# Raw weights and meta products of the first gate pair moved behind its pre-split loads; residual and result stores issued from ScalarE's queue

## The chip, the cores and the metric

The kernel runs on one core of one Trainium2 chip. The metric is the device time of one execution in microseconds: before the change 2130.71 us, the median of three runs (2130.59 to 2131.08). The five engines of the core each take their instructions in a fixed order: TensorE (PE) multiplies matrices, VectorE (DVE), ScalarE (ACT) and GpSimd (POOL) work element by element, SyncE (SP) issues DMA transfers. Any of SP, ACT and POOL can issue a DMA; the issuing instruction stands in that engine's order like any other, and what is behind it waits for it.

## The reference

One layer of a bidirectional encoder is applied to two requests with the same weights, a long one of 1024 tokens and a short one of 512; 16 learned meta tokens stand ahead of each. Cut to what matters here:

```python
D_MODEL = 1024; SEQ = 1024; DEC_SEQ = 512; N_META = 16; D_FF = 2816

def mixer_sublayer(x, ...):                 # two attention groups A and B
    ...
    return x + concat([oa, ob]) @ w_out     # output projection and residual

def conv_glu_sublayer(x, g_ffn, w_ff_gate, w_ff_up, conv_w, conv_b, w_ff_down):
    n = rms_norm(x, g_ffn)
    gate = n @ w_ff_gate
    pad = jnp.pad(gate, ((0, 0), (1, 1), (0, 0)))
    gate = pad[:, :-2] * conv_w[0] + pad[:, 1:-1] * conv_w[1] + pad[:, 2:] * conv_w[2] + conv_b
    return x + (jax.nn.gelu(gate, approximate=False) * (n @ w_ff_up)) @ w_ff_down

def trunk(x, ...):
    h = jnp.concatenate([meta, x], axis=1)
    h = mixer_sublayer(h, ...)
    h = conv_glu_sublayer(h, ...)
    return rms_norm(h, g_final)[:, N_META:]
```

All of it is in float32. The convolution runs over the tokens, so the first real token needs the gate value of the last meta token too.

## The kernel before

**Products.** Activations lie with the 1024 features (or 2816 inner features, 22 column tiles of 128) on the partitions and the tokens along the free axis. A float32 product is made of three faster ones: each operand is split into a rounded part `hi` (a cast on ACT, L114) and the rest `lo` (a subtraction on DVE or POOL, L115), and `mm3` multiplies hi by hi, lo by hi and hi by lo (L121 to L123). So a weight that comes raw from memory costs ACT and DVE a split before PE can use it; some weights are written to memory in split form earlier, while PE is busy with attention, and are then loaded in two parts, `w_hi` and `w_lo`: six of the eight column tiles of w_out (`wo`) and the first pair of column tiles of the gate weight (`wg`).

**Order.** The program is written as Python generators for the two requests, interleaved by hand; a scheduler of the framework, which simulates the engines, then fixes the order in which each engine takes its instructions, from the dependences and from the order of the program. DMA transfers signal their end over one of eight semaphores, taken in turn: a DMA waits until the one before it on its semaphore has landed.

**The stretch that the change touches** has three parts.

1. `mixer_out_long` is the output projection of the long request, in three parts of 340 to 344 tokens (`PARTS`, one piece of each half of the request). For each part it loads the attention output `m` and splits it into `xhi` and `xlo`; then for each of the eight column tiles `j` it loads the weight (`wo` in four blocks at L167, or raw w_out at L150, which is cast on ACT), loads the residual `res` (L712), multiplies (24 matmuls), adds the residual on DVE (L728), **stores the new residual `h`** (L729, read again much later), and adds up squares for the norm (L583; the last two as `sq_p` at L734). The norm itself and the operands that the next stage needs (`combine`: L657, L103 to L107, then casts `x_hi`, `t_hi` and subtractions) are delayed and run inside the next part; those of the third part run inside the gate stage.
2. Beside it the short request ends: `finish` in `conv_glu` scales the result and **stores it as `yT`** (L845), 16 stores of 128 KB in two groups of eight.
3. `conv_glu_long` makes gate and up of the long request, two column tiles (a pair) at a time. Each pair's gate is a Winograd-like scheme of seven products instead of eight (`winograd`), each of 12 matmuls; the first pair takes its operands pre-split from `wg` (L920, five pairs of buffers) and is made in two chunks of tokens, 342 and then 170 in each half, so that the first chunk can start before the third part of the projection is normalised. So the first pair has fourteen products and fourteen loads of two blocks.

**The meta products.** The gate value of the last meta token is made apart, from the *raw* gate weights: for each of the two column tiles ACT multiplies the eight blocks of the weight by the token's normalised values `x0` (`prod`, L970, eight instructions), DVE adds them up (`acc`, L972), and a matmul with two columns sums over the partitions (L989); its result goes into column 0 of `gate` (L990). The convolution starts on ACT (L996, without column 0), two DVE steps add the neighbours (the first one reads column 0), and the GELU follows (L1001). Then come the up products, from raw w_up weights that are split on chip. The raw gate weights have two buffers (`w_f`), shared with the raw w_out tiles of the projection; w_up has two of its own.

In the code before, the raw gate weights of every pair are loaded and the meta products made ahead of that pair's products:

```python
raw = [load_whole(wp, g, g.w_gate[f0 + i]) for i in range(2)]
first_sums = []
for i in range(2):
    ...
for c0, cw in ((0, first), (first, H - first)) if f0 == 0 else ((0, H),):
    for i, half, ps, rest in winograd(g, wp, up, x, raw, c0, cw, g.wg if f0 == 0 else None):
        ...
```

## Time and profile before

| | |
|---|---|
| median of three runs | 2130.71 us |
| the profiled execution | 2127.9 us |
| its span in the profile | 2126.1 us |
| mean granted clock of PE | 0.989 |
| PE busy | 2040.4 us, 96% of the span |
| DVE busy | 1725.0 us, 81% |
| ACT busy | 1156.0 us, 54% |
| POOL busy | 560.8 us, 26% |
| DMA | 296.31 MB, mean 139 GB/s |

The profile is of one execution, and its times are microseconds from the start of its span. In the rows that follow, `PE ps_mm L121 <- DMA w_hi<-wg` is a wait: the PE instruction of line 121 that writes `ps_mm` waited for the DMA that brings `w_hi` from `wg`. A row with a time first is an instruction (or a run of like ones, `x8`): its start, how long it took, engine and line, its output and input, and in brackets how long its engine had been idle before it, and what ended that. `SPq` is SP's queue, where a row is a DMA being issued, not the transfer. A row `1350.00:1375.00` is a stretch of the span: its length, the busy time of each engine with its count of instructions, the clock granted to PE (1.00 is full speed), and the share and rate of the DMA engines.

### The profile page before, as it was taken

Reading aid. Unit: us, or ns where it says so; the run is one execution under the profiler, and the core shown is the slowest. Engines: PE = TensorE matmul, PEld = TensorE weight load, DVE = VectorE, ACT = ScalarE, POOL = GpSimd, SP = SyncE. Lnnn points to the kernel's source line nnn. Section 1 sums busy time; section 2 is a strip of 40 time slices with the busy share of each in tenths; the row PEclk is TensorE's granted clock in tenths of the full one; section 3 lists DMA queues with packets and bytes.
Section 4 is the critical chain, followed back from the end, with each engine's and each line's share of the span. In section 5 each row is a group of like instructions: output and inputs, shape, how many; then the busy total and the mean of one; then the engine's idle time right before and its main releaser. Section 6 shows DMA issues by size and latency. Waiting matters only on the chain.

```text
span 2126.1 us, 35236 instructions
## 1 busy us (share of the span) xinstructions
PE 2040.4 (96%) x12302; PEld 1822.3 (86%) x12302; DVE 1725.0 (81%) x3786; ACT 1156.0 (54%) x2253; POOL 560.8 (26%) x494
## 2 busy tenths in 40 slices
PE   6999999998999999999999999988999999999998
PEld 6988888997887989999989999987887777778877
DVE  6878889767879788888998885578778878879886
ACT  6635566544567556666666765345444444435454
POOL 4653233453112000000000000421544444330112
PEclk9999999999999999999999999999999999999999
DMA  7563435457621322223352225996322232247443
GB/s 255 176 203 130 119 111 171 153 178 236 209 79 56 105 75 67 74 82 118 104 187 88 86 97 147 276 290 217 107 100 90 101 113 84 94 167 260 119 126 127
DMA packets 171426, 296.31 MB, mean 139 GB/s; under 512 B 21456, under 2 KB 90608, under 8 KB 170736
## 3 DMA queue, kind: packets, MB, share of 16 engines
q1 hardware_dynamic: 171248, 294.05, 42.5%
q8 instruction: 97, 1.59, 0.3%
q14 instruction: 81, 0.66, 0.1%
HBM read 211.13 MB, written 82.85 MB: 138 GB/s over the span
## 4 chain that ended last, share of the span: by engine, by line
PE 76%; DVE 12%; DMA 4%; issue 3%; ACT 2%; POOL 1%; SPq 0%; DVEq 0%; ACTq 0%; POOLq 0%
PE ps_mm L121 17%; PE ps_mm L123 17%; PE ps_mm L122 17%; PE ps_t L456 5%; PE ps_s L431 3%; PE ps_s L432 3%; PE ps_s L122 2%; PE ps_s L123 2%; PE ps_s L121 2%; DVE p L433 2%; PE ps_o L471 2%; DVE w_lo L115 1%; PE ps_o L470 1%; DVE acc L972 1%; DMA m<-oT 1%
## 5 line engine op out<-in xcount | busy, mean ns | idle before, releaser
L121 PE MATMUL ps_mm<-xhi,w_hi 128*128 128x258 f32 (+3 forms) x1264 | 383.1, 303 | 12.3 <-ACT xhi L114 5.6
L122 PE MATMUL ps_mm<-xlo,w_hi 128*128 128x258 f32 (+3 forms) x1264 | 378.4, 300 | 0.3 <-POOL xlo L115 0.3
L123 PE MATMUL ps_mm<-xhi,w_lo 128*128 128x258 f32 (+3 forms) x1264 | 377.1, 299 | 0.3 <-DVE w_lo L115 0.3
L433 DVE TENSOR_SCALAR_CACHE_REDUCE p<-ps_s 114x344 f32<-114x344 f32 (+4 forms) x562 | 257.8, 489 | 28.1 <-PE ps_s L432 16.8
L114 ACT CAST pt_hi<-ps_t 128x512 fp32r<-128x512 f32 (+6 forms) x360 | 169.6, 484 | 180.8 <-PE ps_t L456 153.3
L121 PEld LDWEIGHTS ps_mm<-xhi,w_hi 128*128 128x128 f32 x1264 | 239.6, 190 | 18.3 <-ACT xhi L114 7.8
L438 ACT ACTIVATE p<-p,nm 114x1040 f32<-114x1040 f32 (+5 forms) x212 | 214.8, 1013 | 70.5 <-DVE nm L436 69.3
L115 DVE TENSOR_TENSOR w_lo<-w_f,w_hi 128x1024 fp32r<-128x1024 f32 (+1 forms) x182 | 195.2, 1080 | 67.3 <-ACT w_hi L114 66.8
L122 PEld LDWEIGHTS ps_mm<-xlo,w_hi 128*128 128x128 f32 x1264 | 240.0, 190 | 1.9 <-POOL xlo L115 0.8
L123 PEld LDWEIGHTS ps_mm<-xhi,w_lo 128*128 128x128 f32 x1264 | 239.4, 190 | 1.2 <-DVE w_lo L115 0.5
L114 ACT CAST w_hi<-w_f 128x1024 fp32r<-128x1024 f32 (+1 forms) x199 | 167.4, 856 | 79.3 <-PE ps_mm L122 52.2
L115 DVE TENSOR_TENSOR pt_lo<-ps_t,pt_hi 128x512 fp32r<-128x512 f32 (+4 forms) x312 | 172.0, 562 | 42.5 <-ACT pt_hi L114 40.9
L115 POOL TENSOR_TENSOR a_lo<-gate,a_hi 128x256 fp32r<-128x256 f32 x44 | 43.1, 981 | 540.9 <-ACT a_hi L114 521.0
L431 PE MATMUL ps_s<-k,q 128*114 128x348 f32 (+4 forms) x552 | 182.7, 336 | 3.2 <-DVE p L433 3.0
L456 PE MATMUL ps_t<-ident,p 128*128 128x128 f32 (+7 forms) x1188 | 182.4, 269 | 0.9 <-DVE nm L436 0.5
L121 PE MATMUL ps_s<-xhi,w_hi 128*128 128x256 f32 (+4 forms) x480 | 148.2, 311 | 23.2 <-DVE t L333 7.7
L432 PE MATMUL ps_s<-k,q 128*114 128x348 f32 (+4 forms) x552 | 170.3, 313 | 0.0
L456 PEld LDWEIGHTS ps_t<-ident,p 128*128 128x128 f32 (+7 forms) x1188 | 139.9, 135 | 29.1 <-issue 6.8
L123 PE MATMUL ps_s<-xhi,w_lo 128*128 128x256 f32 (+4 forms) x480 | 147.0, 307 | 3.2 <-DMA w_lo<-wo 3.0
L122 PE MATMUL ps_s<-xlo,w_hi 128*128 128x256 f32 (+4 forms) x480 | 148.7, 311 | 1.2 <-DVE xlo L115 0.5
L122 PE MATMUL ps_mm<-t_lo,w_hi 128*128 128x512 f32 (+2 forms) x368 | 142.8, 388 | 1.4 <-DVE t_lo L115 1.4
L121 PE MATMUL ps_mm<-t_hi,w_hi 128*128 128x512 f32 (+2 forms) x368 | 142.8, 388 | 0.0
(273 smaller groups left out, 5269.7 us busy)
## 6 DMA issues: line engine op xcount, KB each, us to landing
w_f<-w_gate SPq DMA_DIRECT2D x46, 512.0 KB, 3.4
w_f<-w_up SPq DMA_DIRECT2D x44, 512.0 KB, 3.3
w_f<-w_in SPq DMA_DIRECT2D x36, 512.0 KB, 4.0
a_f<-act SPq DMA_DIRECT2D x62, 256.0 KB, 2.7
w_f<-w_down SPq DMA_DIRECT2D x22, 512.0 KB, 3.4
act<-a_t SPq DMA_DIRECT2D x44, 256.0 KB, 2.1
a<-w_down SPq DMA_DIRECT2D x40, 256.0 KB, 5.4
w_hi<-wo SPq DMA_DIRECT2D x36, 256.0 KB, 5.2
```

Of the source, the lines that this page charges most:

```text
L114: return (nc.scalar.copy(hi, src).ins, (lo_engine or nc.vector).tensor_tensor(out=lo, in0=src, in1=hi.bitcast(F32), op=ALU.subtract).ins)
L115: (lo_engine or nc.vector).tensor_tensor(out=lo, in0=src, in1=hi.bitcast(F32), op=ALU.subtract).ins)
L121: nc.tensor.matmul(ps, lhsT=whi, rhs=xhi, start=start, stop=False)
L122: nc.tensor.matmul(ps, lhsT=whi, rhs=xlo, start=False, stop=False)
L123: return nc.tensor.matmul(ps, lhsT=wlo, rhs=xhi, start=False, stop=stop).ins
L431: nc.tensor.matmul(ps, lhsT=q[0], rhs=k[:, c0:c0 + cw], start=True, stop=False)
L432: nc.tensor.matmul(ps, lhsT=q[1], rhs=k[:, c0:c0 + cw], start=False, stop=True)
L433: nc.vector.tensor_scalar(out=p[:, c0:c0 + cw], in0=ps, scalar1=HD ** -0.5, scalar2=-3.0e38, op0=ALU.mult, op1=ALU.max, accum_out=mx[:, i: ...
L438: g.last_exp = nc.scalar.activation(p, p, AF.Exp, bias=nm, accum_out=l).ins
L456: nc.tensor.transpose(tps[:, c:c + M], p[:, k0:k0 + kw], g.ident[:M, :M])
L470: nc.tensor.matmul(o, lhsT=v[:, i, :], rhs=hi, start=i == 0, stop=False)
L471: nc.tensor.matmul(o, lhsT=v[:, i, :], rhs=lo, start=False, stop=False)
```

## The change

Three things are edited.

1. The stores of `h` (L729, 24 of them, or eight for each part) and of `yT` (L845, 16) are issued from ACT instead of SP.
2. The raw loads and the meta products become a function, `load_gate`. For every pair but the first it is called where the code stood before. For the first pair it is called after the fourteen products, and what it issues is held, by `behind`, until the last `wg` load has been issued (`g.last_load`). `winograd` no longer gets the raw weights there, which it never used.
3. The raw w_up weights of the first pair are loaded in the same place, behind `wg`, instead of after the GELU in the program's order.

```diff
@@ mixer_out_long @@
-                nc.sync.dma_start(out=halves(g.h[j], o, w),
-                                  in_=h[:, j, :2 * w].rearrange("p (x t) -> p x t", x=2))
+                nc.scalar.dma_start(out=halves(g.h[j], o, w),
+                                    in_=h[:, j, :2 * w].rearrange("p (x t) -> p x t", x=2))
@@ conv_glu, finish @@
-                    nc.sync.dma_start(out=yv[:, k + 1 - ob:k + 1, c0:c0 + cw], in_=y)
+                    nc.scalar.dma_start(out=yv[:, k + 1 - ob:k + 1, c0:c0 + cw], in_=y)
@@ winograd @@
-    a11, a12, a21, a22 = (w[:, i * H:(i + 1) * H] for w in raw for i in range(2))
+    if pre is None:
+        a11, a12, a21, a22 = (w[:, i * H:(i + 1) * H] for w in raw for i in range(2))
+    else:
+        a11 = a12 = a21 = a22 = s2 = None
...
-                nc.sync.dma_start(out=tl.bitcast(F32), in_=pre[i, part, :, half * H:(half + 1) * H])
+                g.last_load = nc.sync.dma_start(out=tl.bitcast(F32), in_=pre[i, part, :, half * H:(half + 1) * H]).ins
@@ conv_glu_long @@
+    def load_gate(f0):
         raw = [load_whole(wp, g, g.w_gate[f0 + i]) for i in range(2)]
-        first_sums = []
+        sums = []
         for i in range(2):
             prod = up.tile([P, KT, P], F32, name="prod", tag="prod", bufs=1)
             for k in range(KT):
                 nc.scalar.activation(prod[:, k], raw[i][:, k * P:(k + 1) * P], AF.Copy, scale=g.x0[:, k:k + 1])
             acc = up.tile([P, P], F32, name="acc", tag="acc")
             nc.vector.tensor_reduce(out=acc, in_=prod.rearrange("p k c -> p c k"), axis=AX.X, op=ALU.add)
-            first_sums.append(acc)
+            sums.append(acc)
+        return raw, sums
+
+    for f0 in range(0, NFF, 2):
+        gate = up.tile([P, 2, N + 1], F32, name="gate", tag="gate", bufs=1)
+        if f0:
+            raw, first_sums = load_gate(f0)
...
+        if f0 == 0:
+            with behind(g, g.last_load):
+                raw, first_sums = load_gate(f0)
+                raw_up = [load_whole(up, g, g.w_up[f0 + i], "w_f2") for i in range(2)]
...
-        raw = [load_whole(up, g, g.w_up[f0 + i], "w_f2") for i in range(2)]
+        raw = raw_up if f0 == 0 else [load_whole(up, g, g.w_up[f0 + i], "w_f2") for i in range(2)]
```

How the engines' orders change is shown at three places. Lines behind the change have 13 more than before (L989 becomes L1002, L996 becomes L1009), L970 becomes L972 and L935 becomes L938. First ACT, from the norm of the projection's third part (L103) to the first casts of the up weights (`w_hi<-w_f_19441`), before:

```order
L103 ACTIVATE rs_y<-ps_s,eps 128x340
L970 ACTIVATE prod<-w_f,x_18439 128x128 x8
L104 ACTIVATE rs_y<-rs_y 128x340
L105 ACTIVATE rstd<-rs_y 128x340
L970 ACTIVATE prod<-w_f,x_18439 128x128 x8
L114 CAST x_hi<-h 128x4x170
L935 COPY u<-ps_mm 128x342
L114 CAST x_hi<-h 128x4x170 x2
L970 ACTIVATE prod<-w_f,x_18439 128x128 x8
L114 CAST t_hi<-h 128x4x170 x4
L935 COPY u<-ps_mm 128x170
L114 CAST w_hi<-w_f_19441 128x512 x2
```

The same engine and place after the change, from the casts of the third part's operands on, with the two conv starts (L1009) and the first casts of the up weights (`w_f_19423`):

```order
L114 CAST t_hi<-h 128x4x170 x4
L938 COPY u<-ps_mm 128x170
L972 ACTIVATE prod<-w_f,x_18439 128x128 x8
L1009 ACTIVATE act<-gate,vec 128x1024 x2
L114 CAST w_hi<-w_f_19423 128x512 x2
L972 ACTIVATE prod<-w_f,x_18439 128x128 x8
L1003 ACTIVATE gate<-ps_mm 128x1
L114 CAST w_hi<-w_s 128x512 x2
```

The two groups of eight meta products stood ahead of and behind the norm; they now stand after it, after the copy from the second chunk's first product, and the second group behind both conv starts and the first two casts of the up weights. (The third group in the rows of before belongs to the second pair.)

Second PE, where the last gate product (`t_hi`, 170 tokens) is followed by the first up product (`x_hi`, 512 tokens), before:

```order
L122 MATMUL ps_mm<-t_lo,w_hi 128x170
L989 MATMUL ps_mm<-ones_d,acc 128x2 x2
L123 MATMUL ps_mm<-t_hi,w_lo 128x170
L121 MATMUL ps_mm<-t_hi,w_hi 128x170
```

And after:

```order
L121 MATMUL ps_mm<-t_hi,w_hi 128x170
L122 MATMUL ps_mm<-t_lo,w_hi 128x170
L123 MATMUL ps_mm<-t_hi,w_lo 128x170
L1002 MATMUL ps_mm<-ones_d,acc 128x2 x2
L121 MATMUL ps_mm<-x_hi,w_hi 128x512
L122 MATMUL ps_mm<-x_lo,w_hi 128x512
```

The two sums over the partitions stood inside the last gate product, ten matmuls before its end; now they stand between that product and the first up product, so that nothing of up can start on PE before both `acc` are made.

Third ACT at the second group of eight result stores, in the projection's third part, before:

```order
L839 ACTIVATE y<-h,gain 128x256 x2
L583 ACTIVATE sq<-h 128x344
L114 CAST xhi<-m 128x340
L114 CAST x_hi<-h 128x4x170 x3
L114 CAST xhi<-m 128x340
L583 ACTIVATE sq<-h 128x344
```

And after:

```order
L114 CAST xhi<-m 128x340
L839 ACTIVATE y<-h,gain 128x256 x2
L845 DMA yT<-y 128x256 x8
L729 DMA h_100<-h 256x1x172
L583 ACTIVATE sq<-h 128x344
L729 DMA h_100<-h 256x1x172
L114 CAST xhi<-m 128x340 x3
L114 CAST w_hi<-w_f 128x512
```

Eight stores of `y` and two of `h` now stand in ACT's order between the scaling of the short request's result (L839) and the casts of the third part's activations (`xhi`).

More of the change, by code (lines that the diff above doesn't have):

```diff
@@ L961, in conv_glu_long @@
     first = PARTS[-1][0]
-    for f0 in range(0, NFF, 2):
-        gate = up.tile([P, 2, N + 1], F32, name="gate", tag="gate", bufs=1)
+    def load_gate(f0):
         raw = [load_whole(wp, g, g.w_gate[f0 + i]) for i in range(2)]
-        first_sums = []
+        sums = []
         for i in range(2):
@@ L972, in conv_glu_long @@
             nc.vector.tensor_reduce(out=acc, in_=prod.rearrange("p k c -> p c k"), axis=AX.X, op=ALU.add)
-            first_sums.append(acc)
+            sums.append(acc)
[4 more added lines that the diff above has]
+            raw, first_sums = load_gate(f0)
         for c0, cw in ((0, first), (first, H - first)) if f0 == 0 else ((0, H),):
-            for i, half, ps, rest in winograd(g, wp, up, x, raw, c0, cw, g.wg if f0 == 0 else None):
+            for i, half, ps, rest in winograd(g, wp, up, x, raw if f0 else None, c0, cw, None if f0 else g.wg):
                 t0 = 1 + half * H + c0
```

## The prediction

> **What bounds the kernel now.** I read the 25 us windows around the changed code first, then the waits of TensorE (PE) there, the chain, and the queue of SyncE (SP).
>
> ```profile
> span 2126.1 us, 35236 instructions
> ...
> core 0: us, PE busy (x) PEld busy (x) DVE busy (x) ACT busy (x) POOL busy (x), PEclk, DMA share, GB/s
> 1350.00:1375.00 25.00, 24.24 (x162) 23.18 (x161) 16.67 (x32) 11.34 (x27) 9.16 (x11) 1.00 0.92 283
> 1375.00:1400.00 25.00, 21.38 (x122) 20.52 (x122) 19.15 (x33) 10.83 (x24) 8.27 (x9) 0.93 0.93 290
> 1400.00:1425.00 25.00, 20.37 (x108) 18.05 (x107) 15.51 (x25) 8.79 (x18) 3.71 (x4) 0.93 0.85 266
> 1425.00:1450.00 25.00, 22.79 (x130) 21.24 (x129) 19.44 (x25) 14.15 (x32) 6.84 (x5) 0.93 0.95 314
> 1450.00:1475.00 25.00, 20.95 (x148) 19.55 (x148) 24.97 (x40) 14.28 (x32) 2.73 (x2) 1.00 0.65 232
> 1475.00:1500.00 25.00, 25.00 (x108) 20.10 (x107) 20.47 (x25) 11.44 (x17) 13.14 (x10) 1.00 0.32 110
> ```
>
> PE is the bound: full from 1475 on. What can be won or lost lies in the four windows from 1375 to 1475, where PE is idle for 3.6 + 4.6 + 2.2 + 4.1 = 14.5 us and its granted clock falls to 0.93. These are the end of the output projection of the long request and the first gate pair. What PE waits for there, from 1320 to 1480:
>
> ```profile
> engine line waited for: us in total, times, longest us
> PE ps_s L121 <- DMA w_hi<-wo: 4.1, 3, 2.5
> PE ps_s L123 <- DMA w_lo<-wo: 3.0, 3, 1.7
> PE ps_s L657 <- ACT sq_p L734: 2.2, 2, 1.3
> PE ps_mm L121 <- DMA w_hi<-wg: 1.9, 1, 1.9
> ...
> PE ps_mm L123 <- DMA w_lo<-wg: 0.7, 1, 0.7
> ```
>
> Mostly weights that come late: `wo` (pre-split w_out) and `wg` (pre-split first gate pair). The queue says why, in SP's rows and one of PE:
>
> ```profile
> 1370.55 5.78 SPq L845 DMA_DIRECT2D yT<-y  x8
> 1376.42 0.52 SPq L729 DMA_DIRECT2D h<-h  x1
> 1377.03 0.56 SPq L167 DMA_DIRECT2D w_hi<-wo  x1
> 1381.91 0.43 PE L121 MATMUL ps_s<-xhi,w_hi 128*128 128x344 f32 x1 [2.53 <-DMA w_hi<-wo]
> ...
> 1406.07 0.33 SPq L150 DMA_DIRECT2D w_f<-w_out  x1
> 1413.30 0.33 SPq L150 DMA_DIRECT2D w_f<-w_gate  x1
> ...
> 1445.70 4.86 SPq L150 DMA_DIRECT2D w_f<-w_gate  x2
> ```
>
> SP issues in order. Eight result stores hold it from 1370.55 to 1376.33, the next weight block goes out at 1377.03, and PE stands 2.53 us for it. From 1406.4 to 1413.3 SP issues nothing: the raw gate weight waits for a free buffer. From 1445.70 it is held 4.86 us by the raw weights of the second gate pair, which wait until the meta products have read the first pair; the `wg` loads behind them are those that PE then misses.
>
> **What the change removes.** All 40 stores leave SP, and the four raw loads of the first pair (w_gate, w_up) go behind the last `wg` load. Two terms.
>
> *Term 1, the output projection.* Its stretch as a whole, and two short windows after idle gaps:
>
> ```profile
> 1362.00:1438.00 76.00, 67.21 (x390) 63.35 (x389) 59.04 (x94) 33.13 (x67) 24.17 (x24) 0.96 0.90 278
> 1382.00:1387.00 5.00, 5.00 (x22) 4.95 (x23) 2.94 (x5) 2.42 (x5) 0.91 (x2) 0.66 1.02 375
> 1410.00:1414.00 4.00, 4.00 (x18) 4.00 (x17) 0.69 (x1) 0.62 (x1) 0.00 (x0) 0.57 0.18 70
> ```
>
> Bound by PE: 76 − 67.2 = 8.8 us idle, and twice 0.34 × 5 = 0.43 × 4 = 1.7 us of slow clock, together 12.2 us. Bound by the transfers: 278 GB/s for 76 us are 21.1 MB; the two raw gate loads (1.05 MB) go, leaving 20.1 MB. At the unchanged share of 0.90 that takes 72.2 us, 3.8 less; at a share of 1.0 (309 GB/s) 65 us, 11 less. Whether freeing SP fills the share is not shown before, so the gain lies between 3.8 and 11; I take the middle, 7.4, as only some of the idle transfer time stands at the two places where SP was held.
>
> *The Trainium skill against this.* The skill's page DMA: Bandwidth & Descriptors (Issuing engines are not separate DMA queues) says that DMAs issued from several engines run on the same 16 DMA engines and that spreading them saves only issue time. By that rule the share stays 0.90 and term 1 is 3.8 us, not 7.4. The trace agrees only in part: the share is already 0.85 to 0.95, but what SP loses here is waiting in order (6.9 us before 1413.3), which is more than issue time.
>
> *Term 2, inside the gate pair.* PE's two waits for `wg`, 1.9 + 0.7 = 2.6 us, go: with no raw load ahead of them, each `wg` load is issued when its buffer comes free, and five pairs of buffers cover the landing. The chain before also shows the meta products between the norm and its use:
>
> ```profile
> 1443.34 2.34 ACT prod L970 x8
> 1445.71 2.01 DVE acc L972
> ...
> 1454.68 1.85 DVE acc L972
> ```
>
> These 6.2 us leave DVE's path to the second chunk's operands. They are worth nothing beyond the 2.6 us in the term: what follows them is term 4, which starts from PE's ninth product, and PE's own pace is late next (seven products of 12 matmuls on the first chunk).
>
> **What the change adds.** *Term 3, ACT.* There is no DMA issue on ACT's queue before. The nearest rows are SP's, 0.52 us for an h store; the eight later y stores cost 3.96/8 = 0.50:
>
> ```profile
> 1388.74 3.96 SPq L845 DMA_DIRECT2D yT<-y  x8
> ...
> yT<-y SPq DMA_DIRECT2D x16, 128.0 KB, 3.3
> ```
>
> 40 × 0.5 = 20 us on ACT, which is busy 33.1 of 76 us: as load this is covered. As order it is not. In the changed program the second eight y stores stand ahead of the casts of the last activations (`xhi`) of the projection's third part. A store waits for its y, and for the completion semaphore that it shares with an earlier transfer: stores five to eight share theirs with the first four, and the two h stores behind with later ones. So ACT can stand for two landings, 2 × 3.3 = 6.6 us. PE's cover is the 24 matmuls of that part which need no late cast: 67.21/390 = 0.17 us each, 4.1 us. The price is between 0 and 6.6 us (cover gone); I take 1.4, near the uncovered rest of 2.5 us but below it, since the first eight stores come where nothing urgent is behind.
>
> *Term 4, the handover from gate to up.* Here a wait is added that the trace of before does not have. Its parts, from rows of before:
>
> ```profile
> 1462.60 0.27 PE L121 MATMUL ps_mm<-t_hi,w_hi 128*128 128x170 f32 x1
> 1463.68 0.38 SPq L920 DMA_DIRECT2D w_hi<-wg  x1
> 1464.16 0.39 SPq L920 DMA_DIRECT2D w_lo<-wg  x1
> 1469.83 0.53 PE L989 MATMUL ps_mm<-ones_d,acc 128*128 128x2 f32 x4
> 1471.39 0.43 PE L121 MATMUL ps_mm<-x_hi,w_hi 128*128 128x512 f32 x1
> ...
> w_f<-w_gate SPq DMA_DIRECT2D x4, 512.0 KB, 3.6
> ...
> 1447.76 2.45 ACT L970 ACTIVATE prod<-w_f,x 128x128 f32<-128x128 f32 x8 [1.18 <-DVE acc L972]
> 1471.50 1.25 ACT L996 ACTIVATE act<-gate,vec 128x1024 f32<-128x1024 f32 x1 [1.08 <-issue]
> 1465.68 0.62 ACT L114 CAST w_hi<-w_f 128x512 fp32r<-128x512 f32 x1
> ```
>
> The last `wg` pair needs the buffer of the ninth of fourteen products, done at 1462.60; its second load is out at 1464.55. Before, PE's first up matmul follows at 1471.39, 8.8 us after the ninth product. In the changed program PE has both meta sums (L989) directly ahead of that matmul, and ACT has the first products, two conv starts (L996), two casts, and only then the second products. Counted from the ninth product: last `wg` load issued at 1.95; raw gate weight landed 3.6 later, 5.55; eight products 2.45, 8.0; two conv starts 2 × 1.25, 10.5; two casts 1.24, 11.7; eight products 2.45, 14.2; the sum on DVE 2.01, 16.2; the meta matmuls 0.53, 16.7. So up starts 16.7 − 8.8 = 7.9 us later against its ninth product, and everything behind it with it, for PE is full from there to the end. PE then stands some ten us, which costs at least one slow-clock stretch more, 1.7 us as in the two windows above: 9.6 us.
>
> On that 1.7 the skill's TensorE: Matmul & The Clock Gate (What's actually happening) says that the clock halves after an idle window of about 3.4 us and returns after a busy one. The trace agrees with its size and not with its threshold: 1.7 us were lost after a gap of 2.53 us. By the page's windows 1.7 to 3.4 us would be an estimate for this gap.
>
> **Sum.** −7.4 − 2.6 + 1.4 + 9.6 = +1.0 us. On the profiled execution of 2127.9 us (span 2126.1 and 1.8 around it) that is 2128.9; the median of the runs, 2130.7, lies 2.8 higher, so 2131.7 there, and I say 2132. A measurement of this kernel can tell about 0.2%, 4.3 us, from no change.
>
> **The rivals.**
> - *ACT's queue becomes the new wait: slower.* Third part of the projection, at the second eight y stores. Price 6.6 instead of 1.4: +6.2, 2136.9. It decides when the casts behind the stores end more than 4.1 us after PE has finished the second part. For it: the stores share semaphores with loads of a stretch in which a landing takes 3 to 5 us, and DVE's work on the first part hangs on casts behind them. Against: ACT is idle more than half of the stretch. Chance 0.18.
> - *The transfers bound the projection, whoever issues them: slower.* Term 1 is 3.8: +4.6, 2135.3. For it: the share of 0.90 with 375 GB/s at the best. Against: the share of 0.18 at 1410, which was SP's doing alone. This is the outcome by the skill's rule on issuing engines. Chance 0.14.
> - *SP freed refills everything: faster.* Term 1 is 11 and term 3 nothing: −4.0, 2126.7; at PE's bound of 12.2, −5.2, 2125.5. For it: two long holds of SP each end in a PE wait. Against: it needs a full share for 65 us. Chance 0.18, counting that the raw gate weight may land earlier than I take.
> - *The change does not reach the waits:* the terms 1 and 2 stay near nothing because loads wait for buffers anyway, while term 4 is paid: +9.6 and up, 2140. Against: the 2.53 us wait began while SP stood at the stores. Chance within the slower ones, 0.05 at most.
>
> **How the numbers follow.** My forecast, the two sides cancelling, has 0.50 and is the "same" case. Slower, the first two rivals, 0.32 with the last in it; faster 0.18. Range: down to 2124 (PE's bound of 2125.5, and the slow-clock stretch of 1.7 at the handover not lost), up to 2140 (the last rival), leaving out about 2 in 10.
>
> **What would show each step.** Term 1: no PE wait of 2.53 us for `w_hi<-wo`, no slow clock there, and the end of the projection some 6 us earlier. Term 2: no wait for `wg`. Term 3: ACT idle at L845 rows and PE waiting for `xhi`. Term 4: PE idle for about ten us ahead of L989, released by DVE's `acc`; if that gap is under 4 us, the forecast is wrong on the fast side. If PE is full at the handover or the stretch from 1362 on gets longer, the argument has failed.

## The result and the profile after

The changed kernel took 2143.74 us (median of six runs, 2142.27 to 2146.63) against 2130.89 of the kernel before in runs beside it: a ratio of 1.0059, with a 95% interval of 1.0042 to 1.0075, or 9 to 16 us more. The forecast was 2132 and its range ended at 2140. Executions of one kernel spread widely here (the one before from 2124.6 to 2139.5 in one set of 35), so below a time counts as a ratio with its interval, and a profile is read by stretches and not by its span. The profiled execution of the changed kernel took 2146.12 us, above its median; its span is 2144.3 us.

The 25 us windows of the changed kernel, with the columns of the prediction's first fence:

```profile
1375.00:1400.00 25.00, 19.14 (x115) 17.79 (x114) 15.60 (x30) 8.09 (x19) 7.84 (x10) 1.00 0.92 291
1400.00:1425.00 25.00, 17.49 (x76) 15.78 (x76) 14.22 (x22) 9.96 (x18) 3.22 (x3) 0.80 0.75 243
1425.00:1450.00 25.00, 20.96 (x117) 18.66 (x116) 18.59 (x29) 9.47 (x17) 8.15 (x4) 0.91 0.78 240
1450.00:1475.00 25.00, 24.09 (x167) 23.64 (x166) 18.46 (x34) 7.31 (x12) 0.00 (x0) 0.95 0.75 239
1475.00:1500.00 25.00, 15.62 (x62) 12.54 (x61) 20.46 (x19) 20.32 (x48) 8.67 (x6) 0.73 0.34 124
```

From 1375 to 1425 PE is busy 36.6 us, where it was busy 41.8 before, and from 1475 to 1500 only 15.6 in place of 25. The transfers were to run fuller; their share falls to 0.75. PE's waits in the changed kernel from 1340 to 1490:

```profile
PE ps_mm L1002 <- DVE acc L974: 9.4, 2, 5.0
PE ps_s L657 <- DVE h L728: 4.0, 1, 4.0
PE ps_s L657 <- ACT sq_p L734: 3.0, 2, 1.6
PE ps_s L121 <- DMA w_hi<-wo: 2.7, 2, 2.1
PE ps_s L121 <- ACT xhi L114: 2.7, 1, 2.7
PE ps_s L122 <- DVE xlo L115: 2.6, 2, 2.4
```

Waits for `wo` and `wg` were at the top before; now it is what ACT and DVE make: `acc`, the residual sum `h`, `xhi`, `xlo`.

To compare kernels whose spans have slipped against each other, I cut at two places that all of them have: **the projection stretch** runs from the first norm's sum (L657, 342 columns) to the last sum of the third norm (L657, `sq_p`), and **the gate stretch** from there to the first up matmul of 512 columns. The windows of these two stretches, before:

```profile
1372.97:1441.26 68.29, 57.83 (x325) 53.36 (x323) 51.91 (x81) 28.64 (x54) 18.62 (x17) 0.95 0.92 291
1441.26:1471.39 30.13, 26.08 (x175) 24.92 (x175) 25.58 (x40) 16.88 (x41) 2.94 (x3) 0.95 0.78 278
```

And after:

```profile
1371.32:1448.52 77.20, 59.79 (x324) 54.70 (x322) 52.08 (x84) 28.45 (x57) 22.89 (x21) 0.91 0.83 264
1448.52:1485.88 37.36, 27.06 (x175) 25.90 (x175) 25.48 (x40) 16.94 (x37) 3.03 (x2) 0.82 0.69 228
```

The projection is 8.9 us longer, the gate stretch 7.2. PE does the same work in both (325 and 324 matmuls in the projection). From the start of up to the end there are 3.7 us more (658.4 against 654.7); two of them are slow clock behind the handover, as shown below. The rest, and 1.7 us less ahead of the first cut, came and went from one profile to the next.

**What happens in the projection.** ACT's rows in the changed kernel, around the two groups of `yT` stores (`ACTq` is ACT's queue, as SPq was SP's):

```profile
1373.25 4.85 ACTq L845 DMA_DIRECT2D yT<-y  x4
1378.15 0.42 ACT L583 ACTIVATE sq<-h 128x256 f32<-128x256 f32 x1 [5.91 <-DMA yT<-y]
1378.23 2.72 ACTq L845 DMA_DIRECT2D yT<-y  x3
...
1396.58 8.27 ACTq L845 DMA_DIRECT2D yT<-y  x8
1406.28 0.49 ACT L583 ACTIVATE sq<-h 128x344 f32<-128x344 f32 x1 [9.85 <-DMA yT<-y]
1406.95 1.23 ACT L114 CAST xhi<-m 128x340 fp32r<-128x340 f32 x3 [0.18 <-issue]
1412.88 0.76 ACT L114 CAST t_hi<-h 128x680 fp32r<-128x680 f32 x1 [1.82 <-DVE h L680]
```

One store takes 0.34 us to issue, eight of them 2.7; the second group holds ACT from 1396.58 to 1404.85, and with the `h` stores behind it ACT computes nothing for 9.85 us. What stands behind it is late: the casts `xhi` of the third part come at 1406.95, the casts `t_hi` of the first part's operands at 1412.88 and later.

The first group does harm too. The first step of the first norm on ACT (L103) stands behind it, and behind a square that waits for a `res` load. It starts 11 us later than before, in the two rows here (the kernel before first):

```profile
1373.82 0.53 ACT L103 ACTIVATE rs_y<-ps_s,eps 128x342 f32<-128x342 f32 x1
1384.91 0.53 ACT L103 ACTIVATE rs_y<-ps_s,eps 128x342 f32<-128x342 f32 x1
```

DVE and PE of the changed kernel in the same stretch:

```profile
1399.77 0.42 PE L122 MATMUL ps_s<-xlo,w_hi 128*128 128x340 f32 x1 [2.42 <-DVE xlo L115]
1407.48 0.59 PE L121 MATMUL ps_s<-xhi,w_hi 128*128 128x340 f32 x2 [2.73 <-ACT xhi L114]
1421.03 0.98 PE L657 MATMUL ps_s<-acc,ones_d 128*128 128x344 f32 x2 [3.96 <-DVE h L728]
...
1395.33 3.96 DVE L842 SCALAR_TENSOR_TENSOR y<-h,gain,rstd 128x256 f32<-128x256 f32 x6
1407.45 1.58 DVE L115 TENSOR_TENSOR xlo<-m,xhi 128x340 fp32r<-128x340 f32 x3 [6.89 <-ACT xhi L114]
1420.37 0.93 DVE L728 TENSOR_TENSOR h<-ps_s,res 128x340 f32<-128x340 f32 x2
```

PE pays for the two groups three times: for `xlo`, for `xhi`, and 3.96 us at the second norm's sum (L657). The wait for `xlo` belongs to the first group, by the engines' orders: ACT had cast its `xhi` at 1395.15, ahead of the second group, but DVE, late with the first norm, had six products for `y` (L842) to make first. The third wait goes a long way round: DVE stands 6.89 us for `xhi`, then works almost without a break, with thirteen us of splits and subtractions ahead of the residual sums (L728, from 1420.37) that PE waits for.

Why eight stores need 8.3 us, the built program says; it lists for each instruction the semaphores that it waits for. The second group in the changed kernel:

```
L845 DMA yT<-y 128x256 [waits DMAHW5_49,DVE_49]
L845 DMA yT<-y 128x256 [waits DMAHW7_49,DVE_49]
L845 DMA yT<-y 128x256 [waits DMAHW1_49,DVE_49]
L845 DMA yT<-y 128x256 [waits DMAHW3_49,Pool_49]
L845 DMA yT<-y 128x256 [waits DMAHW5_49,DVE_49]
...
```

Since SP's loads take every other semaphore (DMAHW0 to 7), the eight stores have four among them: the fifth waits for the landing of the first, and so on. The trace shows the same four semaphores twice; it has the first store issued at 1396.58 and the fifth at 1401.93, 5.35 us later, just behind the first one's landing; a landing took 3.5 to 5.3 us in this group. On SP before, the eight had a semaphore each.

**What happens at the handover** is what term 4 said, in rows of SP, ACT, DVE and PE in the changed kernel, and a window:

```profile
1467.01 0.27 PE L121 MATMUL ps_mm<-t_hi,w_hi 128*128 128x170 f32 x1
...
1468.23 0.38 SPq L923 DMA_DIRECT2D w_lo<-wg  x1
1468.66 0.90 SPq L150 DMA_DIRECT2D w_f<-w_gate  x2
...
1475.36 2.44 ACT L972 ACTIVATE prod<-w_f,x 128x128 f32<-128x128 f32 x8 [9.19 <-DMA w_f<-w_gate]
1477.71 2.36 ACT L1009 ACTIVATE act<-gate,vec 128x1024 f32<-128x1024 f32 x2
1479.97 1.12 ACT L114 CAST w_hi<-w_f 128x512 fp32r<-128x512 f32 x2
1481.00 2.44 ACT L972 ACTIVATE prod<-w_f,x 128x128 f32<-128x128 f32 x8
...
1483.47 1.90 DVE L974 TENSOR_REDUCE acc<-prod 128x128 f32<-128x1024 f32 x1 [0.50 <-ACT prod L972]
...
1479.81 0.59 PE L1002 MATMUL ps_mm<-ones_d,acc 128*128 128x2 f32 x2 [4.35 <-DVE acc L974]
1485.43 0.59 PE L1002 MATMUL ps_mm<-ones_d,acc 128*128 128x2 f32 x2 [5.03 <-DVE acc L974]
1485.88 0.77 PE L121 MATMUL ps_mm<-x_hi,w_hi 128*128 128x512 f32 x1
...
1476.00:1488.00 12.00, 3.16 (x9) 2.69 (x10) 8.81 (x8) 11.02 (x31) 3.72 (x3) 0.51 0.47 168
```

The order is the predicted one: eight products, conv starts, two casts, eight products, the sum on DVE, PE. The first row is where the tenth product takes over from the ninth. PE idles 9.4 us, and its clock is at 0.51 for these 12 us; it is still at 0.50 from the first up matmul (1485.88) to 1489.8, which costs two us more behind the second cut.

### The profile page after: what moved, and what is told of

The parts are those of the page before. It is cut to its first block, busy times and chain, and to the rows that moved or that the text cites. A ratio compares the mean times of both kernels' runs of the same rounds, so it can differ in the third digit from the quotient of the medians.

```text
span 2144.3 us, 35234 instructions
## 1 busy us (share of the span) xinstructions
PE 2047.4 (95%) x12302; PEld 1827.7 (85%) x12302; DVE 1722.3 (80%) x3786; ACT 1154.6 (54%) x2253; POOL 565.0 (26%) x494
## 5 line engine op out<-in xcount | busy, mean ns | idle before, releaser
L123 PE MATMUL ps_mm<-xhi,w_lo 128*128 128x258 f32 (+3 forms) x1264 | 377.2, 299 | 0.0
L123 PEld LDWEIGHTS ps_mm<-xhi,w_lo 128*128 128x128 f32 x1264 | 239.7, 190 | 0.9 <-DVE w_lo L115 0.2
L123 PE MATMUL ps_s<-xhi,w_lo 128*128 128x256 f32 (+4 forms) x480 | 147.4, 308 | 0.5 <-DMA w_lo<-wo 0.5
L123 PE MATMUL ps_mm<-t_hi,w_lo 128*128 128x512 f32 (+2 forms) x368 | 142.8, 388 | 0.2 <-DMA w_lo<-wg 0.2
```

The costliest lines, as they stand in the source:

```text
L123: return nc.tensor.matmul(ps, lhsT=wlo, rhs=xhi, start=False, stop=stop).ins
```

## The experiments

**The theories.** Q: a store in ACT's order waits for landings and holds up ACT's casts; this and the handover (H) are two costs, and the gain in the projection is small. Against Q stands T: the transfers bound the projection, whoever issues them. Against both: all of the loss is the handover.

Each kernel's median (e5 and e8 follow in the text), its ratio to the kernel before in runs beside it, and from its one profile the two stretches, in us:

| kernel | median | ratio (95%) | projection | gate |
|---|---|---|---|---|
| before (profile) | 2127.9 | | 68.3 | 30.1 |
| changed | 2143.74 | 1.0059 (1.0042 to 1.0075) | 77.2 | 37.4 |
| e1_stores | 2139.41 | 1.0038 (1.0023 to 1.0052) | 74.2 | 34.6 |
| e2_gate | 2137.18 | 1.0033 (1.0020 to 1.0046) | 67.4 | 38.3 |
| e3_ystores | 2136.52 | 1.0030 (1.0018 to 1.0041) | 76.7 | 31.0 |
| e4_hstores | 2132.61 | 1.0006 (0.9991 to 1.0020) | 68.4 | 35.7 |
| e6_ypool | 2137.54 | 1.0022 (1.0003 to 1.0040) | 68.3 | 30.9 |
| e7_y256 | 2134.03 | 1.0009 (0.9995 to 1.0024) | 67.4 | 36.1 |
| e9_meta_behind | 2132.45 | 1.0011 (0.9998 to 1.0025) | 67.2 | 32.7 |
| e10_up_first | 2135.30 | 1.0024 (1.0013 to 1.0035) | 66.7 | 26.8 |
| e11_after_y256 | 2132.45 | 1.0006 (0.9994 to 1.0017) | 66.1 | 35.4 |
| e12_after_up_first | 2141.30 | 1.0054 (1.0041 to 1.0067) | 76.7 | 27.2 |
| f1_no_y | 2127.15 | 0.9985 (0.9972 to 0.9997) | 68.2 | 30.5 |
| f2_y256_late | 2131.09 | 1.0011 (0.9995 to 1.0026) | 67.7 | 29.7 |
| f3_y256_sp_late | 2130.38 | 1.0001 (0.9990 to 1.0012) | 64.8 | 29.9 |
| f4_ypool_again | 2133.78 | 1.0021 (1.0005 to 1.0038) | 67.8 | 32.6 |

A hundredth of a per cent is 0.2 us. The gate stretch also varies with the slow clock that a profile happens to catch in it (0.75 in e7's, where PE is busy 32.7 of the 36.1 us, 0.95 before), so it tells less than the projection. e4 and e7, whose handover is that of before, show 35.7 and 36.1 there.

**e1, e2: the two halves of the change.** e1 is the kernel before with both stores on ACT; e2 is the changed kernel with both back on SP:

```diff
e1:
-                nc.sync.dma_start(out=halves(g.h[j], o, w),
+                nc.scalar.dma_start(out=halves(g.h[j], o, w),
...
-                    nc.sync.dma_start(out=yv[:, k + 1 - ob:k + 1, c0:c0 + cw], in_=y)
+                    nc.scalar.dma_start(out=yv[:, k + 1 - ob:k + 1, c0:c0 + cw], in_=y)
e2: the same lines the other way round, in the changed kernel
```

> The kernel before, with both kinds of stores (h and yT) issued from ACT, and the first pair's raw weights left where they were. Theory Q (stores block ACT's queue): ACT stands at the two groups of yT stores for about 7.6 and 8.3 us as in the changed kernel, the last sum of the projection (L657) comes about 7 us later than the 1441.3 of before, and the time is 5 to 8 us above before. Rival T (the transfers bound the projection, whoever issues them): within 2 us of before. Rival H (all of the loss is the handover from gate to up): within 2 us of before or some us faster.

> The changed kernel with both kinds of stores back on SP, so that only the first pair's raw weights and meta products are moved. Theory Q with the handover as the second cost: PE waits 7 to 10 us for acc ahead of the first up product, and the projection, without the raw gate weight in SP's order, ends up to 4 us sooner than before: 3 to 8 us above before. Rival H: all of it, 11 to 14 us above before. If the handover costs nothing by itself (its wait only follows from the late projection): within 2 us of before or faster.

The stores alone cost 8.1 us (4.9 to 11.1) and lengthen the projection by 5.9, with the changed kernel's waits of PE (4.2 us for `h`, 2.0 for `xhi`, 1.7 for `xlo`); the gate half alone costs 7.0 (4.3 to 9.8), lengthens the gate stretch by 8.2 and shortens the projection by 0.9. So neither "the handover alone" nor "the transfers, whoever issues" stands: each half costs about what Q and H say, and their sum, 15, lies inside the interval of the whole change (9 to 16).

**e3, e4: which stores?** The kernel before with only the `yT` stores, or only the `h` stores, on ACT (the first or the second pair of lines of e1's diff alone).

> The kernel before with only the 16 yT stores issued from ACT. Theory Q, with the yT groups as the cause: ACT stands 5 to 9 us at each group, PE then waits for xhi and for the norm, 4 to 8 us above before. If the h stores do the harm: within 2 us of before. If SP, freed of the two groups (4.9 to 5.8 and 4.0 us), wins more than ACT loses: 2 to 4 us below before.

> The kernel before with only the 24 h stores issued from ACT. Theory Q, with the yT groups as the cause: single stores whose data is there cost 0.5 us each and stand where ACT is idle, so within 2 us of before. If single h stores hold ACT too, by the transfer before them on their semaphore: 2 to 6 us above before.

The `yT` stores cost 6.4 us (3.8 to 8.7) and the projection is 76.7; the `h` stores 1.3 (-1.9 to 4.3), with a projection as before. In e3 ACT stands at the stores as in the changed kernel, but PE's waits (from the first cut to the second) look different from what I had written down:

```profile
PE ps_s L123 <- DMA w_lo<-wo: 5.9, 5, 4.4
PE ps_s L121 <- DMA w_hi<-wo: 5.3, 4, 2.7
PE ps_s L657 <- ACT sq_p L734: 3.2, 2, 2.0
PE ps_s L657 <- DVE h L728: 1.2, 1, 1.2
PE ps_s L121 <- ACT xhi L114: 1.0, 1, 1.0
```

Eleven us are waits for weights (7.1 before), only 1.0 for `xhi`. The shared semaphores work in both directions. Each transfer takes the next of the eight; in e3's program a load of `res` and one of `w_lo<-wo` on SP wait for the semaphores that the second and the third store of ACT's first group took. Such a load waits until ACT has come to the store and the store has landed, and what stands behind it on SP waits too. The trace shows both directions: SP issues an `h` store, that `res` and that `w_lo` at 1379.20, 1381.18 and 1381.74, each within 0.1 us of the landing of ACT's first, second and third store (1379.14, 1381.16, 1381.68), and ACT's fifth, sixth and seventh store go out within 0.1 us of the landings of three loads of SP. How much of the price goes this way and how much over ACT's casts, no run separates.

**e7: by count or by bytes?** As e3, with two column tiles in each store:

```diff
-                y = op.tile([P, ob, cw], F32, name="y", tag="y", bufs=YB if s == 1 else 4) if k % ob == 0 else y
+                y = op.tile([P, 2, cw], F32, name="y", tag="y", bufs=YB if s == 1 else 4) if k % 2 == 0 else y
...
-                if (k + 1) % ob == 0:
-                    nc.sync.dma_start(out=yv[:, k + 1 - ob:k + 1, c0:c0 + cw], in_=y)
+                if k % 2:
+                    nc.scalar.dma_start(out=yv[:, k - 1:k + 1, c0:c0 + cw], in_=y)
...
-YB = 12
+YB = 6
```

> The kernel of the run e3_ystores (only yT stores on ACT) with 8 stores of 256 KB in place of 16 of 128 KB, in as much buffer space. Theory Q, by count (each store waits for the landing before it on its semaphore): four stores of a group each have a semaphore of their own, ACT stands 2 to 4 us in place of 9 to 10 at each group, and the time is 0 to 3 us above before. Rival, by bytes (the stores take their time in the DMA engines): as in e3_ystores, 4 to 7 us above before.

1.9 us above before (-1.1 to 5.1), and the projection is 67.4 in place of e3's 76.7, with the same bytes. ACT's second group in e7:

```profile
1388.48 3.41 ACTq L845 DMA_DIRECT2D yT<-y  x4
```

Four stores issue in 3.4 us where the changed kernel's eight took 8.3. It is the count and not the bytes: four stores have a semaphore each.

**e6 and f4: the stores on POOL.** `nc.gpsimd.dma_start` in place of `nc.sync.dma_start` for `yT`, in the kernel before, in two sets of runs. Its stores have completion semaphores of their own.

> The kernel before with only the 16 yT stores issued from POOL, whose transfers have completion semaphores of their own. Theory Q (what costs is the place in ACT's order and the semaphores that ACT's stores share with SP's loads): POOL may stand, but neither ACT nor SP does; the 2.5 us wait of PE behind the first group goes, and the time is 0 to 5 us below before. Rival S (taking the stores out of SP's order lets other transfers collide, whoever issues the stores): as with the yT stores on ACT (e3_ystores), 4 to 7 us above before.

> The kernel of e6_ypool again (yT stores on POOL), for a second profile: 3 of its 12 runs lay at 2124 to 2131 and 9 at 2136 to 2143, and the profile was of a fast one. A run of the upper group should show where the 7 to 15 us go: in the projection, as with stores on ACT (its stretch 74 us and more in place of 68.3), or in slow clock somewhere else (the stretch at 68).

The projection is as before in both profiles (68.3 and 67.8), so moving stores out of SP's order does no harm there by itself, but nor does it gain: PE's 2.5 us wait is gone and others are there. The times are not what I expected. Their spread is wide (2124.42 to 2143.42), and their ratios are 1.0022 (1.0003 to 1.0040) and 1.0021 (1.0005 to 1.0038). Both profiles were of executions at the low end, so where the others lose 3 to 13 us stays open.

**e5, e8, e9: the handover.** e9 is e2 with the first up products made ahead of the meta sums on PE:

```diff
+        ready = []
+        if f0 == 0:
+            ups = winograd(g, wp, up, x, raw_up, 0, H)
+            ready.append(next(ups))
         for i in range(2):
             ps = g.psum.tile(P, 2, "mm")
             nc.tensor.matmul(ps, lhsT=first_sums[i], rhs=g.ones_d[:, 0:2], start=True, stop=True)
...
-        raw = raw_up if f0 == 0 else [load_whole(up, g, g.w_up[f0 + i], "w_f2") for i in range(2)]
-        for i, half, ps, rest in winograd(g, wp, up, x, raw, 0, H):
+        if f0:
+            raw = [load_whole(up, g, g.w_up[f0 + i], "w_f2") for i in range(2)]
+            ups = winograd(g, wp, up, x, raw, 0, H)
+        for i, half, ps, rest in chain(ready, ups):
```

> The kernel of e2_gate (stores on SP, gate loads moved) with the two meta sums behind the first two up products of the first pair, and nothing else changed. Theory H (PE waits for acc): the 7.5 us wait is gone, and what is left is a wait of about 4 us for the up weights' casts, which stand behind the first eight meta products and the conv starts on ACT: 4 to 9 us below e2_gate (2128 to 2133). Rival (the casts come as late as acc did): within 2 us of e2_gate's 2137.

Before it came e5, with `for ... in (*ready, *ups)` in place of the last line, and e8, which is e5 with the `yT` stores on POOL:

> The kernel of the run e2_gate (raw weights and meta products of the first pair moved, all stores on SP), with the two meta sums placed on PE behind the first up products instead of ahead of them. Theory H (the handover costs what PE waits for acc): the wait of 7.5 us ahead of up goes, and some slow clock with it, so 6 to 10 us below e2_gate: 2127 to 2131. Rival: the up weights' own casts, behind the meta products in ACT's order, come just as late, and PE waits for w_hi instead: within 2 us of e2_gate (2137).

> The kernel of e5_late_meta with the yT stores issued from POOL: neither of the two costs of the changed kernel, and what it was meant to free is free. If both theories hold, the gains add up: 2 to 8 us below before (2123 to 2129). If PE's waits for wo and wg come from the transfers alone: within 2 us of before.

Written so, all seven up products of a pair are listed ahead of the additions that read them, for every pair, and the buffers of the partial sums are written again before they are read: the up values of the long request are not the reference's, and the order differs in all eleven pairs. Their 2128.10 (0.9988, 0.9974 to 1.0002) and 2128.53 (0.9990, 0.9976 to 1.0003) answer another question, and e9 asks mine again.

e9 came out 2.3 us above before (-0.4 to 5.3) against e2's 7.0; the intervals overlap. In the profile the wait for `acc` is gone, and what is left ahead of the first up matmul in e9 is the wait for the up weights' casts:

```profile
PE ps_mm L121 <- ACT w_hi L114: 3.0, 1, 3.0
```

The second cut hides a part of it, though. The 30 us behind the first up matmul, before and in e9:

```profile
1471.39:1501.39 30.00, 30.00 (x130) 24.14 (x129) 25.47 (x31) 14.84 (x25) 15.77 (x11) 1.00 0.31 105
1475.23:1505.23 30.00, 28.12 (x107) 22.33 (x108) 29.90 (x30) 17.49 (x41) 11.94 (x8) 0.88 0.24 84
```

There e9 loses 1.9 us to a wait for `w_lo`, the split of a later up weight, and 3.6 to slow clock (0.12 of 30): 5.5 us, where before lost none and e2 loses 2.4 (0.92). With the gate stretch that makes 8.1 us over before for e9 and 10.6 for e2. So the wait for `acc` is gone, but three quarters of the price stayed, as waits for the up weights' splits and as slow clock.

**e10, e12: the up weights first.** e10 is e9 with `load_gate` for the first pair called behind `ready.append(next(ups))`, so that the raw up weights are loaded and cast ahead of the gate's; e12 is the same in the changed kernel, with the stores on ACT.

> As e9_meta_behind, and the raw up weights are loaded and cast ahead of the raw gate weights and the meta products. Theory H in full: neither acc nor the casts hold PE, so up starts within 3 us of the last gate product; 6 to 13 us below e2_gate and 0 to 6 us below before (2125 to 2131). Rival (the landing of the up weights behind the last wg load is late by itself, so PE waits for them in place of acc): 2132 to 2137.

> The changed kernel, its stores left on ACT, with the handover of e10_up_first. If the handover is the other separate cost: 5 to 10 us below the changed kernel (2134 to 2139), which is what the stores alone cost in e1_stores or less. If the late projection hides the handover: within 2 us of the changed kernel (2142 to 2146).

A miss, and instructive. The gate stretch falls to 26.8 and 27.2, below before, and yet e10 is 5.1 us above before (2.8 to 7.5). PE's meta sums in e10 now stand behind two up products:

```profile
1477.67 0.38 PE L1007 MATMUL ps_mm<-ones_d,acc 128*128 128x2 f32 x2 [0.80 <-DVE acc L974]
1482.10 0.54 PE L1007 MATMUL ps_mm<-ones_d,acc 128*128 128x2 f32 x2 [4.04 <-DVE acc L974]
```

The wait has moved by two products. From the start of up to the end e10 takes 664.8 us against 654.7; 4.8 of these ten are the two waits and some 2.7 slow clock around them (0.89 from 1470 to 1495); the rest was not traced further. The raw gate weights are loaded last now, and in PE's order the sums must come before the rest of up. e12 says that most of the changed kernel's loss stays when only the handover is reordered: 11.5 us above before (8.7 to 14.3), with a projection of 76.7. At 2141.30 it lies between the two outcomes written down for it.

**e11, f2, f3: the store cost out, then the handover reordered too.** e11 is the changed kernel with e7's larger stores (on ACT); f2 adds e9's order; f3 is f2 with all stores on SP.

> The changed kernel with 8 yT stores of 256 KB on ACT in place of 16 of 128 KB; the handover is left as it is. If the stall of ACT at the 16 stores is one of two separate costs: 3 to 7 us below the changed kernel (2137 to 2141), and ACT stands 3 to 4 us at each group. If the two costs overlap (one hides behind the other): within 2 us of the changed kernel (2142 to 2146).

> The changed kernel with both costs taken out: 8 yT stores of 256 KB on ACT (e11_after_y256), and the meta sums behind the first two up products (e9_meta_behind). If the two costs are separate, the gain of e9 over e2 (4.7 us) comes on top of e11's 2132.5: 2126 to 2130, faster than both kernels. If not: 2131 to 2134.

> As f2_y256_late, but with all stores on SP: what the larger stores and the handover bring without any store on ACT. If a freed SP is worth something: 1 to 4 us above f2_y256_late. If SP's queue was never the bound: within 1.5 us of it.

Only the size of the stores differs between e11 and the changed kernel, and 11 of its 12.6 us are gone: 1.3 us above before (-1.3 to 3.6), more than either outcome written down for it. e11's two stretches:

```profile
1379.00:1445.12 66.12, 57.56 (x325) 52.03 (x323) 51.53 (x83) 28.34 (x55) 19.07 (x19) 0.95 0.90 288
1445.12:1480.54 35.42, 25.89 (x174) 24.66 (x175) 26.53 (x41) 17.04 (x37) 2.87 (x2) 0.91 0.79 267
```

The projection is 11.1 us shorter than the changed kernel's. The gate stretch keeps the wait for `acc` (8.7 us in e11) and 5.3 of its 7.2 us. The handover's price doesn't show in e11's median as it does in e2's, 2137.18 with the same order; that difference, about 5 us, I can't account for. The two ran in different sets; in their one profile each, PE's clock is at half for 17 us around e2's handover (1465.0 to 1482.1) and for ten around e11's (1474.2 to 1484.4), but whether the other runs did so isn't known.

f2 and f3 are within the error of before, 1.0011 and 1.0001: there is no gain on either queue. Nor is the handover's cost wholly out: in the 30 us behind the first up matmul f2 loses 5.4 us, like e9, and f3 3.7. Counted so, the handover still costs f2 about five us and e11 about seven, and e11's shorter projection makes up the difference, so f2 is not faster than e11. No version that computes the whole layer beat the kernel before.

**f1: what SP's holds were worth.** The kernel before without most of the `yT` stores:

```diff
-                if (k + 1) % ob == 0:
+                if (k + 1) % ob == 0 and k in (0, KT - 1):
```

> The kernel before, leaving out 12 of the 16 yT stores (only column tiles 0 and 7 of the short request are written). SP is then neither held by the stores nor are their bytes moved. If SP's holds at the stores were what the predicted gain of the projection rests on (7.4 us): the stretch from the first sum of the norms (L657) to the last falls from 68.3 to 62 to 64 us, and the time by 4 to 7 us. If PE waits there for weights that are held by their buffers and by the transfers anyway: the stretch falls by 0 to 2.5 us, and the time by no more than 3.

3.2 us less (0.6 to 6.0), but the projection is 68.2 in place of 68.3, and both stretches together 98.7 in place of 98.4: leaving out twelve of the sixteen transfers altogether gains nothing there. (In f1 the last two tiles' sums come in one run of four matmuls from 1438.25; the cut is its third, at 1439.55.) Where the 3.2 us of the medians come from, the profile doesn't say. PE's waits in f1's two stretches begin:

```profile
PE ps_s L657 <- ACT sq_p L734: 5.6, 1, 5.6
PE ps_s L121 <- DMA w_hi<-wo: 3.2, 3, 2.1
PE ps_mm L121 <- DMA w_hi<-wg: 2.6, 2, 2.3
```

The `wo` waits shrink from 7.1 to 5 us (L123's 1.8 among them), and the next thing in line, the squares of the last tiles, takes 5.6.

## Why the prediction was wrong

**Terms 3 and 1 failed, terms 2 and 4 held in the main.** The projection stretch got longer, which the prediction itself had named as the sign that its argument failed. By its steps, for the profiled executions:

| term | predicted | measured |
|---|---|---|
| 1, projection, SP freed and two loads gone | -7.4 | -0.6 and -2.2 (f2, e11); -0.9 to -3.5 with the loads moved alone (e2, e9, e10, f3) |
| 3, stores in ACT's order | +1.4, at most 6.6 | +5.9 (e1 less before, a freed SP counted in), +9.3 (e3 less e7), +11.1 (changed less e11) |
| 1 and 3 together, projection stretch | -6.0 | +8.9 |
| 2 and 4, gate stretch | -2.6 + 9.6 = +7.0 | +7.2, and 2.0 of slow clock behind it |

*Term 3* is the step that made the forecast miss. Its mechanism was written down: stores that share semaphores, casts behind them, the second group. Four things in it were wrong. The landing was taken as 3.3 us, the median on SP; with the stores on ACT it is 4.7, and the fifth store waits for one in full. The place was priced by one wait, for `xhi`, against a cover of 4.1 us; PE paid at three places, and the dearest (3.96 us) is reached over DVE's order: the late `xhi`, the splits and subtractions behind it, L728, L657. The first group was priced at nothing, as one behind which nothing urgent stands; the first norm stood there, and started 11 us late. And the way back, from ACT's stores to SP's loads over the common semaphores, was not seen. "The price is between 0 and 6.6 us" was thus no bound: the comparisons give 5.9 to 11.1. The first rival, with a chance of 0.18, had the place and the sign; its price of 6.6 us is near the low end.

*Term 1* took the middle between 3.8 and 11 where less than the lower end was to be had. Its bounds came from PE's idle time and the share of the transfers, as if one long hold of SP were one long loss. f1 shows otherwise: with most of the stores left out, the projection gains 0.1 us, and other waits come up behind the `wo` wait of 2.53 us. The kernels with the raw loads moved and the stores on SP (e2, e9, e10) gain 0.9 to 1.6, the one with larger stores on SP as well (f3) 3.5. The share of the DMA engines in that stretch was 0.88 to 0.93 in all kernels without the stall, and above 0.93 in none, whether SP was free or not. What the Trainium skill says in DMA: Bandwidth & Descriptors (Issuing engines are not separate DMA queues), that another issuing engine brings no more transfer, agrees with this: the share did not rise. SP had 40 issues fewer, and the stretch still got 8.9 us longer: the wait in order on ACT outweighed whatever that saved. The rival drawn from it had the better term 1 (3.8), but by itself came to 2135.3, since it kept term 3 at 1.4.

*Terms 2 and 4* had the mechanism right: PE was to stand "some ten us" ahead of the meta sums and stood 9.4. Term 2 came to 2.8 us where 2.6 were forecast: from the last sum of the projection to the end of the ninth product it is 18.5 us (1448.52 to 1467.01), where it was 21.3 before. Term 4 was too small. From the ninth product to the first up matmul it is 18.9 us (1467.01 to 1485.88), where 16.7 were forecast and 8.8 stood before. The raw gate weight is the reason: its load is issued at 1468.66 and the first product starts at 1475.36, 6.7 us in place of 3.6, with four loads of 512 KB going out together. Up thus starts 10.1 us later against its ninth product, not 7.9, and the slow clock behind its start costs 2.0 more: about 12 in place of 9.6. That 7.0 and 7.2 agree in the table is luck, since the forecast's 7.0 has the slow clock in it and the measured 7.2 has not that behind the cut. (Of the 6.2 us that the prediction takes off DVE's path, 2.34 are ACT's; its sum does not use them.)

e9 bears out the path: with the sums behind the first up products the wait for `acc` goes and the gate stretch falls from 38.3 to 32.7. But 3.1 us of these 5.6 come back within the next 30 us, and e10 says the same: the wait can be moved but not removed by reordering PE alone, as long as the raw weights are loaded behind `wg`.

The sum in the medians: 12.6 us (9 to 16), of which the stores alone make 8.1 and the gate half alone 7.0. The profiled executions lie 18.2 apart, because the changed one was above its median and the one before below.

**Still open:** why e11 is about 5 us faster than e2 with the same handover, so that the handover's price in the time rests on e2 alone; what f1's 3.2 us are; which share of the stall's price goes over ACT's casts and which over SP's loads; and where the upper runs with stores on POOL lose.

## What to carry to other kernels

A DMA is an instruction in its engine's order: before moving stores to another engine's queue, count how many stand in a row, which completion semaphores they share with the other queue's transfers, and what compute stands behind them; fewer and larger stores (four of 256 KB in place of eight of 128 KB) took the harm out here. A queue that stands still is only worth freeing if PE's next wait is far behind: leave the transfers out altogether once, and see what the stretch gains. When a wait is moved, look behind the place where a stretch is cut, too. Price a late operand along every engine's order that it passes through, not only at its first reader.

## What the runs showed of the hardware

The clock of PE falls to half around short gaps: in the changed kernel it is at 0.51 over the whole of 1476 to 1488, with gaps of 4.35 and 5.03 us in it, and in the kernel before it fell behind a gap of 2.53 us (0.66 from 1382 to 1387). That last one is shorter than the idle window of about 3.4 us that the Trainium skill gives in TensorE: Matmul & The Clock Gate (What's actually happening). Also not expected: the time from issue to landing of a 128 KB store went from a median of 3.3 us on SP to 4.7 on ACT's queue, and for 256 KB it was 6.9 us in e11, yet four of the latter held ACT for less than eight of the former.
